# Fox layer on one core: weights split once for two token halves, h tiles loaded ahead on SP's queue, eight staging tiles

## The chip, the cores and the metric

The kernel runs on one core of one Trainium2 chip. The metric is the time on the device in microseconds; the kernel before took 2207.94 us (median of 3 runs, 2205.89 to 2215.18). The profile shown is of one further execution, which took 2212.18 us.

## The reference, cut to what matters

One layer (DEPTH is 1), so only the FoX mixer and the MLP run. S = 512 tokens, D = 2048, 16 heads of 128, MLP width 8192, all float32:

```
h = rmsnorm(x, g0)
q, k, v, f_pre = split(h @ w_in)                  # 2048 x (3 * 2048 + 16)
cum = cumsum(log_sigmoid(f_pre + b_f))            # per head, along the tokens
p = softmax(q k^T / sqrt(128) + cum_i - cum_j, causal)
x = x + rmsnorm(concat_heads(p @ v) @ w_out, g1)  # w_out 2048 x 2048
h = square(relu(rmsnorm(x, g2) @ w1))             # w1 2048 x 8192
x = x + rmsnorm(h @ w2, g3)                       # w2 8192 x 2048
```

## The kernel before, in words

**Split operands.** Every float32 operand of a large product is split in two: `hi` is the value cast to float32r on ScalarE, `lo` is value minus `hi`, subtracted on VectorE. A product is then three matmuls, hi x hi, hi x lo and lo x hi (`mm3`, lines 95 to 97; `mm3b`, lines 465 to 467). For weights of 128 x 1024 `load_split` issues the load on SP's queue (line 88) and does the cast (line 89) and the subtraction (line 90). Split operands stand in one large SBUF tile, `opr`, by column numbers that the code computes; raw weights wait in three tiles.

**Attention and output projection.** A loop over 16 heads multiplies q and k of one head while scores, transposes and values of the head before are slipped between the units. The result of a head is copied to `o32`; heads 0 to 9 (`KEEP = 10`) keep it in SBUF, heads 10 to 15 store it to the DRAM tile `od` (line 359) and load it again in `split_o` (line 399), which splits it (lines 401 and 402). The output projection has four groups of 512 columns (`NC = 4`), each with 8 weight tiles (`kb`), and accumulates four tiles of 128 tokens in PSUM. The last column group runs twice, once for each token half, and loads and splits its 8 weight tiles each time. During the second pass the first half is normalised (`norm1`, `residual`, `norm2`), stored to `x2d` by SP (line 527) and, at kb 6 and 7, transposed by `turn` (line 543).

**Plain tiles of the MLP.** The first 512 columns of w1 are multiplied plainly (`plain`), 8 weight tiles for each token half. The second pass keeps the split weights of three tiles and loads and splits the other five again. While it runs, `turn(1, p)`, `mix` and `split_mix` build the seven operands per pair of 128-row blocks of the input that the rest needs.

**The rest of the MLP, by Strassen-like sevens.** Columns of w1 come in pairs of 128 (30 pairs here); a pair of two-by-two blocks is multiplied with seven products in place of eight. `load_seven` loads four blocks of a weight (512 KB, SP, line 456) into one of four staging tiles of `spool`, forms three sums on VectorE (lines 457 to 459) and splits all seven (lines 440 and 441) into one of three places in turn (`tplaces`). One such weight is one step: 7 products x 2 x 3 = 42 matmuls. The first half (`ps`) takes 4 steps per pair and stores the squared relu in seven-form to DRAM (`hd`, line 693). The second half (`po`) goes over five blocks (`ci`) of six pairs (`CHUNK`), each with four column groups (`cp`): 24 steps per block. The h tile of a pair is loaded back by `want` (line 676, GpSimd's queue, one buffer `h7`) and split into one of eight places (`NRING`) of `opr`; six are in use in a block, two are spare. At the end of each column group seven PSUM banks are copied to `st` tiles (line 822, six buffers of `w2pool`) and stored to the DRAM tile `md`, from the second block on with accumulation (lines 824 and 826, GpSimd's queue). In the last block `gather` (line 773) reads the products of a finished column group back, two tiles of 896 KB which take staging tiles of `spool`, and adds them to `acc`; the gather of the last group, the last plain products (`pz`), the norm and the output follow the loop.

**Order.** All is written as straight code, with the slipped-in work placed by hand. On each engine's queue the instructions stand in the order that the scheduler of the language gave them; it follows the code, but takes an instruction that is free ahead of one that isn't.

## Time and profile before

| | us |
|---|---|
| median of 3 runs | 2207.94 |
| the profiled execution | 2212.18 |
| its span (first to last instruction) | 2210.4 |
| TensorE busy in it | 2130.7 (96%) |
| VectorE busy | 1498.8 (68%) |
| ScalarE busy | 953.0 (43%) |
| GpSimd busy | 267.9 (12%) |
| mean granted clock of TensorE, share of full speed | 0.985 |

The span is 1.78 us shorter than the profiled execution, which is 4.24 us above the median. Busy time of TensorE is from matmuls in a pipeline. By the granted clock TensorE ran at full speed nearly throughout. The stages: attention up to about 650 us, the output projection to 820, the plain tiles to 880, the first MLP half to 1494, the second to 2150, the tail to the end.

### The profile page before, as it was taken

The page shows a single profiled execution, that of the slowest core. Times are in us where ns is not written, and L with a number is a line of the kernel's source. Part 1 is how long each engine was busy: PE and PEld are TensorE (multiplying, and loading weights), DVE is VectorE, ACT ScalarE, POOL GpSimd, SP SyncE. Part 2 cuts the span into 40 slices and gives each one's busy share as a digit, 9 for nine tenths or more (in the row PEclk, how much of TensorE's full clock was granted, in tenths as well). Part 3 has the DMA queues.
Part 4 walks back from the last instruction along what each step waited for, and adds up shares of the span by engine and source line. Part 5 has one row for each costly group of instructions (what it writes and reads, how often), then busy time and mean ns, then how long its engine had stood idle before and what let it go on. Part 6 is the DMA issues. An engine that isn't in the chain of part 4 may idle for free. (4 is left out here: it accounts for less than half of the span.)

```text
span 2210.4 us, 34770 instructions
## 1 busy us (share of the span) xinstructions
PE 2130.7 (96%) x14450; PEld 1979.9 (90%) x14450; DVE 1498.8 (68%) x2004; ACT 953.0 (43%) x1138; POOL 267.9 (12%) x350
## 2 busy tenths in 40 slices
PE   8999999999989998999999999998999999999896
PEld 7788888888878878999999999998999999999885
DVE  9553453543543368888888888887687767767676
ACT  4433332333332365444444444445454555445352
POOL 8000000000010000000000000001112221222123
PEclk9999999999999999999999999999999999999998
DMA  5332232233343363544444444456567877877777
GB/s 175 110 95 82 93 95 89 95 93 103 91 152 99 121 229 124 179 162 163 150 156 163 162 144 163 162 167 211 196 218 194 217 205 183 225 182 197 190 206 225
DMA packets 103662, 346.12 MB, mean 157 GB/s; under 512 B 11712, under 2 KB 15936, under 8 KB 99024
## 3 DMA queue, kind: packets, MB, share of 16 engines
q1 hardware_dynamic: 72048, 232.42, 32.7%
q0 software_dynamic: 31312, 111.46, 18.6%
q8 instruction: 113, 1.85, 0.3%
q14 instruction: 45, 0.37, 0.1%
q10 hardware_dynamic: 144, 0.02, 0.0%
HBM read 264.65 MB, written 79.20 MB: 156 GB/s over the span
## 5 line engine op out<-in xcount | busy, mean ns | idle before, releaser
L466 PE MATMUL po<-opr 128*128 128x256 f32 x1204 | 344.7, 287 | 18.5 <-DVE opr L441 18.4
L465 PE MATMUL po<-opr 128*128 128x256 f32 x1204 | 341.1, 286 | 6.2 <-ACT opr L440 6.0
L467 PE MATMUL po<-opr 128*128 128x256 f32 x1204 | 340.4, 285 | 1.1 <-DVE opr L441 1.1
L465 PE MATMUL ps<-opr 128*128 128x256 f32 x1120 | 318.3, 284 | 6.6 <-ACT opr L440 6.6
L466 PE MATMUL ps<-opr 128*128 128x256 f32 x1120 | 318.1, 284 | 0.0
L467 PE MATMUL ps<-opr 128*128 128x256 f32 x1120 | 317.5, 284 | 0.2 <-DVE opr L441 0.2
L466 PEld LDWEIGHTS po<-opr 128*128 128x128 f32 x1204 | 234.2, 195 | 21.8 <-DVE opr L441 21.7
L465 PEld LDWEIGHTS po<-opr 128*128 128x128 f32 x1204 | 232.4, 194 | 7.8 <-ACT opr L440 7.0
L467 PEld LDWEIGHTS po<-opr 128*128 128x128 f32 x1204 | 232.6, 194 | 1.5 <-DVE opr L441 1.3
L465 PEld LDWEIGHTS ps<-opr 128*128 128x128 f32 x1120 | 216.2, 193 | 6.8 <-ACT opr L440 6.8
L466 PEld LDWEIGHTS ps<-opr 128*128 128x128 f32 x1120 | 216.3, 193 | 0.0
L467 PEld LDWEIGHTS ps<-opr 128*128 128x128 f32 x1120 | 215.8, 193 | 0.5 <-DVE opr L441 0.5
L441 DVE TENSOR_TENSOR opr<-seven_a,opr 128x1792 fp32r<-128x1792 f32 x80 | 161.9, 2024 | 51.5 <-ACT opr L440 50.2
L440 ACT CAST opr<-seven_b 128x1792 fp32r<-128x1792 f32 x86 | 145.1, 1693 | 115.5 <-PE po L467 88.2
L440 ACT CAST opr<-seven_a 128x1792 fp32r<-128x1792 f32 x80 | 134.8, 1685 | 139.0 <-PE ps L466 133.4
L441 DVE TENSOR_TENSOR opr<-seven_b,opr 128x1792 fp32r<-128x1792 f32 x86 | 173.7, 2020 | 19.8 <-ACT opr L440 19.6
L457 DVE TENSOR_TENSOR seven_b<-seven_b 128x512 f32<-128x512 f32 x120 | 82.6, 688 | 125.5 <-DMA seven_b<-in_w2s 125.1
L465 PE MATMUL ps<-opr,w 128*128 128x256 f32 x560 | 158.5, 283 | 0.0
L466 PE MATMUL ps<-opr,w 128*128 128x256 f32 x560 | 158.5, 283 | 0.0
L467 PE MATMUL ps<-opr,w 128*128 128x256 f32 x560 | 158.5, 283 | 0.0
L465 PE MATMUL po<-w,opr 128*128 128x256 f32 x476 | 136.3, 286 | 3.5 <-ACT w L440 2.3
L466 PE MATMUL po<-w,opr 128*128 128x256 f32 x476 | 136.2, 286 | 1.8 <-DVE w L441 1.8
(233 smaller groups left out, 5233.1 us busy)
## 6 DMA issues: line engine op xcount, KB each, us to landing
seven_a<-in_w1s SPq DMA_DIRECT2D x120, 512.0 KB, 3.6
seven_b<-in_w2s SPq DMA_DIRECT2D x120, 512.0 KB, 4.3
md<-st POOLq DMA_DIRECT2D x140, 256.0 KB, 8.4
hd<-ev POOLq DMA_DIRECT2D x30, 1024.0 KB, 4.4
h<-hd POOLq DMA_DIRECT2D x30, 896.0 KB, 5.2
raw_o<-in_wo SPq DMA_DIRECT2D x40, 512.0 KB, 3.5
raw_q<-in_wq SPq DMA_DIRECT2D x32, 512.0 KB, 3.7
raw_k<-in_wk SPq DMA_DIRECT2D x32, 512.0 KB, 3.7
```

The lines of the kernel that those rows point to most:

```text
L440: nc.scalar.copy(hi, z)
L441: nc.vector.tensor_tensor(out=lo, in0=z, in1=f32(hi), op=ALU.subtract)
L457: nc.vector.tensor_tensor(out=raw[:, 4:6], in0=raw[:, 1:3], in1=raw[:, 0:1].to_broadcast([P, 2, 256]), op=ALU.add)
L465: nc.tensor.matmul(o, a[0], b[0], start=start, stop=False, skip_group_check=True)
L466: nc.tensor.matmul(o, a[0], b[1], start=False, stop=False, skip_group_check=True)
L467: nc.tensor.matmul(o, a[1], b[0], start=False, stop=stop, skip_group_check=True)
```

## The change

- `KEEP`, `od` and its stores and loads go: every head's result keeps a tile of its own in SBUF. `cb`, the row of sums of a head, has one buffer in place of two.
- The last column group of the output projection splits its 8 weight tiles once, into places `OPLACE` of `opr` that stay for both token halves. The plain tiles split all 8 weight tiles once, into `PPLACE`; the first token half takes them in the order `EARLY`, the second from 0 to 7.
- The split inputs move within `opr`; `split_mix` writes two pieces (256 and 768 columns), each with a cast and a subtraction.
- `want` becomes `h_load` (SP's queue) and `h_split`, called by `h_steps` at given steps counted from the start of a block. Tiles 1 and 3 of the first block are loaded into staging tiles of `spool`, the others into the one `h7` tile. The places of h in `opr` follow `HSLOT`. The first step of the MLP sevens starts with the third of the three places for split weights.
- The order of the four weights of pair 2 is 0 to 3.
- `st` has eight buffers. `gather` of groups 0 and 1 is called two column groups later at their first step, that of group 2 after the loop.

```diff
-    def load_split(src, name, pieces=1, between=None):
-        wplace[0] += 1
-        at = WBASE + wplace[0] % 3 * 2048
+    def load_split(src, name, pieces=1, between=None, at=None):
+        if at is None:
+            wplace[0] += 1
+            at = WBASE + wplace[0] % 3 * 2048
...
-                cb = ap_.tile([P, S], F32, tag="cb", name=f"cb_{h}", bufs=2)
+                cb = ap_.tile([P, S], F32, tag="cb", name=f"cb_{h}")
...
-                if h < KEEP:
-                    o32[h] = ap_.tile([P, S], F32, tag=f"o32_{h}", name=f"o32_{h}")
-                    nc.scalar.copy(o32[h], ps)
-                    return
-                o = ap_.tile([P, S], F32, tag="o32", name=f"o32_{h}", bufs=4)
-                nc.scalar.copy(o, ps)
-                nc.sync.dma_start(od[h], o)
+                o32[h] = ap_.tile([P, S], F32, tag=f"o32_{h}", name=f"o32_{h}")
+                nc.scalar.copy(o32[h], ps)
...
+        OPLACE = [20480, 22528, 24576, 26624, 18432, WBASE, WBASE + 2048, WBASE + 4096]
+        w_last = {}
         def out_unit(py, c, kb, ts=range(TT)):
-            w = load_split(wo[c, kb], f"o{c}_{kb}")
+            if c < NC - 1:
+                w = load_split(wo[c, kb], f"o{c}_{kb}")
+            else:
+                if kb not in w_last:
+                    w_last[kb] = load_split(wo[c, kb], f"o{c}_{kb}", at=OPLACE[kb])
+                w = w_last[kb]
...
         def split_mix(p, m4):
-            hi, lo = opr[:, p * 2560 + 256:p * 2560 + 1280], opr[:, p * 2560 + 1536:p * 2560 + 2560]
-            nc.scalar.copy(hi, m4)
-            nc.vector.tensor_tensor(out=lo, in0=m4, in1=f32(hi), op=ALU.subtract)
+            for at, n, c in ((p * 1024 + 256, 512, slice(0, 256)), (RB + p * 1536, 768, slice(256, 1024))):
+                w = c.stop - c.start
+                hi, lo = opr[:, at:at + w], opr[:, at + n:at + n + w]
+                nc.scalar.copy(hi, m4[:, c])
+                nc.vector.tensor_tensor(out=lo, in0=m4[:, c], in1=f32(hi), op=ALU.subtract)
...
+        EARLY = [5, 6, 7, 4, 0, 1, 2, 3]
+        PPLACE = [18432, WBASE, WBASE + 2048, WBASE + 4096, RB, RB + 2048, RB + 4096, RB + 6144]
...
         def plain(hf, p):
-            order = LATE if hf else range(8)
-            if hf == 0 or p < 5:
-                w[p] = load_split(w1p[p], f"a{hf}_{p}")
+            order = range(8) if hf else EARLY
+            if hf == 0:
+                w[p] = load_split(w1p[p], f"a_{p}", at=PPLACE[EARLY.index(p)])
...
+    tplace[0] = 1
...
-    def want(n):
-        if n >= NSTR:
-            return
-        h7 = h_tile(f"h7_{n}")
-        nc.gpsimd.dma_start(h7, hd[n, :, 256:2048].rearrange("p (n c) -> p n c", c=256))
-        at = n % NRING * 2 * SLOT
-        hops[n] = split7(h7, [opr[:, at + i * SLOT:at + (i + 1) * SLOT] for i in range(2)])
+    HSLOT = [0, 3, 6, 1, 2, 4, 5, 7]
+    hraw = {}
+    def h_load(n):
+        hraw[n] = seven(f"h7_{n}") if n in (1, 3) else h_tile(f"h7_{n}")
+        nc.sync.dma_start(hraw[n], hd[n, :, 256:2048].rearrange("p (n c) -> p n c", c=256))
+    def h_split(n):
+        at = HSLOT[n % NRING] * 2 * SLOT
+        hops[n] = split7(hraw[n], [opr[:, at + i * SLOT:at + (i + 1) * SLOT] for i in range(2)])
+    def h_steps(i):
+        for ci in range(NSTR // CHUNK):
+            if ci == 0:
+                splits, loads = [-3, -2, -1, 0, 1, 2], [-4, -4, -3, -2, -1, 1]
+            else:
+                splits, loads = [-16, -11, -5, -3, -1, 2], [-18, -13, -7, -5, -3, 0]
+            for k in range(CHUNK):
+                if i == ci * 4 * CHUNK + splits[k]:
+                    h_split(ci * CHUNK + k)
+            for k in range(CHUNK):
+                if i == ci * 4 * CHUNK + loads[k]:
+                    h_load(ci * CHUNK + k)
...
-        w2pool = w2s_.enter_context(tc.tile_pool(name="w2pool", bufs=6, reuse_waits="tile"))
+        w2pool = w2s_.enter_context(tc.tile_pool(name="w2pool", bufs=8, reuse_waits="tile"))
...
-                    if ci == 0 and cp == 0 and k < 3:
-                        want(k + 3)
-                    elif ci > 0 and cp == 0 and k in (0, 2):
-                        want(n0 + 4 + k // 2)
-                    if cp in (1, 2) and k == 2:
-                        want(n0 + CHUNK + cp - 1)
-                    if cp == 3 and k in (2, 4):
-                        want(n0 + CHUNK + 1 + k // 2)
+                    h_steps((ci * 4 + cp) * CHUNK + k)
...
-                        if cp > 0 and k == 5:
-                            gather(cp - 1, ep, seven)
+                        if cp > 1 and k == 0:
+                            gather(cp - 2, ep, seven)
...
+        gather(2, ep3, lambda name: big(name)[:, 0:7])
         gather(3, ep3, lambda name: big(name)[:, 0:7])
```

## Rows read from the trace of the kernel before

**Rows 1.** Page, part 1: engine, busy us (share of the span) xinstructions.

```profile
PE 2130.7 (96%) x14450; PEld 1979.9 (90%) x14450; DVE 1498.8 (68%) x2004; ACT 953.0 (43%) x1138; POOL 267.9 (12%) x350
```

**Rows 2.** Busy time by stage: from:to length, engines (xinstructions), clock, DMA share, GB/s.

```profile
580.00:640.00 60.00, 60.00 (x293) 50.63 (x292) 34.47 (x60) 25.64 (x50) 7.02 (x13) 1.00 0.36 110
640.00:680.00 40.00, 33.48 (x142) 27.15 (x141) 12.38 (x17) 10.52 (x16) 2.13 (x4) 0.91 0.46 141
...
780.00:820.00 40.00, 35.08 (x175) 29.08 (x174) 26.63 (x46) 23.04 (x47) 4.30 (x8) 0.96 0.72 249
...
860.00:900.00 40.00, 28.63 (x207) 27.34 (x207) 36.94 (x53) 22.17 (x30) 1.63 (x3) 0.87 0.52 193
900.00:1480.00 580.00, 580.00 (x4836) 580.00 (x4835) 493.79 (x666) 259.64 (x202) 14.93 (x28) 1.00 0.47 156
1488.00:1540.00 52.00, 44.57 (x336) 43.35 (x335) 39.18 (x45) 26.44 (x22) 6.42 (x12) 0.93 0.63 210
...
1640.00:2020.00 380.00, 370.19 (x3049) 367.79 (x3048) 284.04 (x310) 188.68 (x173) 85.06 (x103) 1.00 0.77 201
2020.00:2147.00 127.00, 113.13 (x870) 110.19 (x869) 87.29 (x118) 52.52 (x49) 25.11 (x28) 0.95 0.74 199
```

**Rows 3.** Timeline of PE: start, us, what [idle before <- releaser].

```profile
659.97 0.79 PE L95 MATMUL py<-opr 128*128 128x512 f32 x1 [5.33 <-ACT opr L401]
...
805.42 0.50 PE L95 MATMUL py<-opr 128*128 128x512 f32 x1 [2.89 <-ACT opr L89]
...
886.70 0.58 PE L465 MATMUL ps<-opr 128*128 128x256 f32 x1 [6.62 <-ACT opr L440]
...
1518.66 0.39 PE L465 MATMUL po<-opr 128*128 128x256 f32 x1 [1.77 <-ACT opr L440]
...
2082.61 0.58 PE L466 MATMUL po<-opr 128*128 128x256 f32 x1 [4.62 <-DVE opr L441]
```

**Rows 4.** Waits, whole span: who <- whom: us in total, times, longest.

```profile
ACT opr L401 <- DMA o<-od: 9.0, 2, 7.7
...
POOL h L676 <- DVE opr L441: 226.9, 29, 11.5
...
ACT opr L440 <- DMA h<-hd: 78.9, 17, 8.6
...
ACT st L822 <- DMA md<-st: 50.4, 18, 4.8
...
PE ph L97 <- DVE opr L90: 4.5, 4, 1.6
```

**Rows 5.** Groups by line: what xcount | busy us, mean ns | idle before.

```profile
L441 DVE TENSOR_TENSOR opr<-h,opr 128x1792 fp32r<-128x1792 f32 x30 | 60.6, 2021 | 6.3 <-ACT opr L440 6.3
...
L440 ACT CAST opr<-h 128x1792 fp32r<-128x1792 f32 x30 | 50.8, 1692 | 83.8 <-DMA h<-hd 78.9 <-PE po L466 4.9
...
L90 DVE TENSOR_TENSOR opr<-raw_a,opr 128x1024 fp32r<-128x1024 f32 x13 | 15.9, 1221 | 3.9 <-PE ph L96 1.9 <-ACT opr L89 1.7
```

**Rows 6.** Page, part 6: DMA issues, KB each, median us to landing.

```profile
seven_b<-in_w2s SPq DMA_DIRECT2D x120, 512.0 KB, 4.3
md<-st POOLq DMA_DIRECT2D x140, 256.0 KB, 8.4
...
h<-hd POOLq DMA_DIRECT2D x30, 896.0 KB, 5.2
```

**Rows 7.** Timeline of SP, output projection and plain tiles.

```profile
790.05 3.96 SPq L527 DMA_DIRECT2D x2d<-yg  x6
...
865.97 23.33 SPq L456 DMA_DIRECT2D seven_a<-in_w1s  x5
```

**Rows 8.** Timeline of DVE behind the loop.

```profile
2170.71 0.43 DVE L776 TENSOR_TENSOR m<-m 128x256 f32<-128x256 f32 x1 [8.85 <-DMA m<-md]
```

**Rows 9.** Timeline of POOL at the start of the second MLP half.

```profile
1513.03 0.53 POOL L676 DMA_DIRECT2D h<-hd  x1 [6.42 <-DVE opr L441]
1522.89 0.53 POOL L676 DMA_DIRECT2D h<-hd  x1 [9.34 <-DVE opr L441]
```

More of the change, by code (lines that the diff above doesn't have):

```diff
@@ L33 @@
 CHUNK = 6
-KEEP = 10
 WARM = 9
@@ L161, in fox_layer @@
     cumd = dpool.tile([H, S], F32, name="cumd")
-    od = dpool.tile([H, P, S], F32, name="od")
     with ExitStack() as att:
@@ L395, in split_o @@
         def split_o(h):
[L396 to L399 removed]
+            o = o32[h]
             ah, al = act_pair()
@@ L474, in xop @@
             at, step = RA + p * 1024 + i * 256, 512
+        elif i < 4:
+            at, step = p * 1024 + (i - 2) * 256, 512
         else:
-            at, step = p * 2560 + (i - 2) * 256, 1280
+            at, step = RB + p * 1536 + (i - 4) * 256, 768
         return opr[:, at:at + 256], opr[:, at + step:at + step + 256]
@@ L557, in turn @@
                 nc.scalar.activation(x4[:, 512 + 256 * i:768 + 256 * i], ps[:, 256 * i:256 * (i + 1)], AF.Copy, scale=gc[:, 1, k:k + 1])
-            at = p * 2560
+            at = p * 1024
             nc.scalar.copy(opr[:, at:at + 512], x4[:, 512:1024])
-            nc.vector.tensor_tensor(out=opr[:, at + 1280:at + 1792], in0=x4[:, 512:1024], in1=f32(opr[:, at:at + 512]), op=ALU.subtract)
+            nc.vector.tensor_tensor(out=opr[:, at + 512:at + 1024], in0=x4[:, 512:1024], in1=f32(opr[:, at:at + 512]), op=ALU.subtract)
             return x4
@@ L627, in plain @@
                 else:
-                    at = p * 2560 + (256 if kh == 0 else 0)
-                    b = opr[:, at:at + 256], opr[:, at + 1280:at + 1536]
+                    b = xop(p, 3 - kh)
                 for f in range(4):
@@ L632, in plain @@
                     mm3(ph[f][:, cols], a, b, p == order[0] and kh == 0, p == order[-1] and kh == 1)
-        for p in range(8):
-            plain(0, p)
-            if p == 0:
-                norm1(1)
-            if p < 4:
-                residual(1, p)
-            if p == 3:
-                norm2(1)
-            if p >= 4:
-                store_x2(1, p - 4)
-        x4, m4 = {}, {}
-        for i in range(3):
-            x4[i] = turn(1, LATE[i])
-            if i < 2:
-                m4[i] = mix(LATE[i], x4[i])
-        for i in range(8):
-            plain(1, LATE[i])
-            split_mix(LATE[i], m4[i])
-            if i + 2 < 8:
-                m4[i + 2] = mix(LATE[i + 2], x4[i + 2])
-            if i + 3 < 8:
-                x4[i + 3] = turn(1, LATE[i + 3])
+        for i in range(8):
+            plain(0, EARLY[i])
+            if i == 0:
+                norm1(1)
+            if i < 4:
+                residual(1, i)
+            if i == 3:
+                norm2(1)
+            if i >= 4:
+                store_x2(1, i - 4)
+        x4, m4 = {}, {}
+        for p in range(3):
+            x4[p] = turn(1, p)
+            if p < 2:
+                m4[p] = mix(p, x4[p])
+        for p in range(8):
+            plain(1, p)
+            split_mix(p, m4[p])
+            if p + 2 < 8:
+                m4[p + 2] = mix(p + 2, x4[p + 2])
+            if p + 3 < 8:
+                x4[p + 3] = turn(1, p + 3)
     first.close()
@@ L724, in fox_layer @@
             b = [(psum_att if n % 2 else psum_acc)(f"ps_{n}_{i}") for i in range(4)]
-            order = [3, 2, 0, 1] if n == 2 else range(4)
-            for g in order:
+            for g in range(4):
                 w = load_seven(w1s[n - 2, g], f"a{n}_{g}")
@@ L731, in fox_layer @@
                         mm3b(b[bi][:, part * 256:(part + 1) * 256], [zz[:, BOF[j], kk * P:(kk + 1) * P] for zz in w], xop(2 * g + kk, AOF[j]),
-                             g == order[0] and kk == 0 and FIRST[bi] == j, g == order[-1] and kk == 1)
-                if n == 2 and g in order[1:3]:
-                    evac_plain(order.index(g) - 1)
-                if n == NPAIR - 1 and g > 0:
-                    want(g - 1)
+                             g == 0 and kk == 0 and FIRST[bi] == j, g == 3 and kk == 1)
+                if n == 2 and g in (1, 2):
+                    evac_plain(g - 1)
+                if n == NPAIR - 1:
+                    h_steps(g - 4)
             evac_seven(b, n)
@@ L747, in last_w @@
         nc.sync.dma_start(raw, w2p[i // 2, i % 2])
-        hi, lo = opr[:, i * 2048:i * 2048 + 1024], opr[:, i * 2048 + 1024:i * 2048 + 2048]
+        at = [0, 10752, 21504, 23552, 2048, 4096, 6144, 8192][i]
+        hi, lo = opr[:, at:at + 1024], opr[:, at + 1024:at + 2048]
         nc.scalar.copy(hi, raw)
```

13 lines of the change are left out of this document (4 added, 9 removed).

## The prediction

> **What bounds the kernel now.** The reader starts with the shares of the engines on the page: TensorE is busy for 2130.7 of 2210.4 us [rows 1], so what a change can win is its idle time, about 80 us, and what the clock loses beside it. The second view is the busy time by stage [rows 2]. In the first half of the MLP (900 to 1480 us) TensorE is never idle: 4836 matmuls in 580 us, 0.12 us each, so one step (one weight tile, 7 products x 2 x 3 matmuls = 42) takes 5.04 us. The same holds up to 640 us. The loss sits in six places, each read as the stage's length less the busy time, and as the stage's length times what the granted clock lacks (mean clock 0.91 over 40 us: at most 3.6 us of full-speed work lost; between the levels of 1.2 and 2.4 GHz the clock falls after the idle places and comes back): end of attention (640 to 680) 6.5 idle + 3.6 clock; last columns of the output projection (780 to 820) 4.9 + 1.6; end of the plain tiles and hand-over to the MLP (860 to 900) 11.4 + 5.2; start of the second MLP half (1488 to 1540) 7.4 + 3.6; its middle (1640 to 2020) 9.8 + 0; its end (2020 to 2147) 13.9 + 6.4. Together about 54 us idle and 20 us of clock. The rest, behind 2147, is the tail, in which VectorE waits 8.85 us for the last gathered products [rows 8].
>
> The third view, the idle times of TensorE one by one [rows 3], names who ends each: a cast of ScalarE (L401) at 660, a cast of w_out (L89) at 805, a cast of a MLP tile (L440) at 886 and at 1518, the subtraction behind it (L441) at 2082. ScalarE is itself only 43% busy, so the fourth view asks what it waits for [rows 4]: 9.0 us for `o<-od`, 78.9 us for `h<-hd`, 50.4 us for `md<-st` to free a staging tile.
>
> **Part 1: heads 10 to 15 stay in SBUF.** Six stores and six loads of 256 KB go, and with them the waits of L401. The idle 5.33 us at 660 ends with that cast [rows 3], and the 9.0 us say that it waited for the loads [rows 4]. What is late next is the chain of head 15 (copy, cast, subtraction): it hangs on the value matmuls, which stand three units ahead of its use, each 48 matmuls long. I take 9.5 of the 10.1 us; bounds 6 and 10. The room is paid with one `cb` tile in place of two: the load of a head's row of sums then starts when VectorE has read the row of the head before, still a head's matmuls ahead of its use. TensorE is full there (60.00 of 60 us [rows 2]), so I take nothing. Were the cover gone, 15 loads of 256 KB, each below the 4.3 us that 512 KB take [rows 6], would be at most 65 us.
>
> **Part 2: w_out's last columns and the plain tiles are split once.** For the second token half 8 loads, 8 casts and 8 subtractions of w_out go, and 5 of each of the plain tiles (13 subtractions of 1.22 us [rows 5], 16 us of VectorE, and 13 casts). At 780 to 820 TensorE waits for just these: SP issues six `x2d` stores at 790 to 794 [rows 7], which wait for VectorE, ahead of the last two loads of w_out; the idle 2.89 us at 805 [rows 3] follows. In the new kernel no load stands there: 4.9 + about 1 of clock, 6 us in all (bounds 3 and 6.5). In the plain tiles' second pass 4.5 us of waits for L90 [rows 4] go, since no L90 is left in it. VectorE is busy for 36.94 of 40 us there [rows 2]; it loses 5 x 1.22 and gains 8 more instructions by the two-piece `split_mix`: from 0.43 us for 256 columns, 1.22 for 1024 and 2.02 for 1792 [rows 5, 8] an extra instruction costs some 0.16 us, 1.3 in all, so VectorE is ahead by 4.8 us. The hand-over at 886 (6.62 us) [rows 3] waits for the first MLP tile, whose load SP issues only at 865.97 [rows 7], behind the plain loads that now go; its first split now has a place that is free early (`tplace` starts at the third). But its sums still share VectorE with the last `split_mix`: I take half, 3.3 us, and 3 of the 5.2 us of clock. 4.5 + 3.3 + 3 = 11 (bounds 4 and 16). The new places of x, h and the last weights in `opr`, and the plain order of the first MLP steps, change no instruction's size; a place that came free too late would show as a cast waiting for TensorE, and I take nothing for it. Part 2 gives 17 us.
>
> **Part 3: h loads ahead, on SP's queue.** Before, an h tile is loaded when the one before it has been split (one buffer): GpSimd's queue waits 226.9 us for that in 29 of 30 loads [rows 4]. At the start of the second half the issues at 1513.03 and 1522.89 [rows 9] are 9.9 us apart, a step is 5.04: h tiles 2 to 5 can't keep up, and TensorE idles 7.4 us. Now tiles 1 and 3 use the weights' staging tiles, so two loads of six no longer hang in that chain. What is late next is VectorE: six subtractions of 2.02 us [rows 5] beside the weights' work, 39.18 of 52 us [rows 2], and two of four staging tiles are lent out. Of 11 us I take 7 (bounds 0 and 10). Later h tiles still have one buffer, so there the load can't start earlier than before; what changes is the ring: `md<-st` takes 8.4 us to land and stood ahead of h on GpSimd's queue (h: 5.2) [rows 6].
>
> **Part 4: eight staging tiles.** Seven copies leave PSUM at the end of each column group; with six tiles the seventh waits for the first store, 50.4 us in 18 waits, 2.8 each [rows 4], and every cast queued behind it on ScalarE waits too. With eight the seven copies of a group fit, and the next group comes six steps, 30 us, later. Split weights have three places, so ScalarE is at most two steps ahead of TensorE, and 2.8 us less is as much as most of the idle times there. Parts 3 and 4 in the middle: 7 of 9.8 us (bounds 1 and 9.8). At the end: the gathers of column groups 0 and 1 move to a step where their products have long landed, and group 2's leaves the loop; but each still takes two of four staging tiles, for which the loads of weights wait (the 4.62 us at 2082 [rows 3]), and now stands beside seven stores. Of 20.3 us I take 8 (bounds -3 and 15).
>
> **Part 5: the tail.** Group 2's gather (two loads of 896 KB, 14 additions of 0.43 us) now falls behind the loop, into the 8.85 us [rows 8] in which VectorE waits anyway, but its loads share the DMA engines with the last stores, which are on the path. Loads of h's size take 5.2 us [rows 6]; hidden they cost nothing, both in a row 10 us. I take 3 us lost.
>
> **The sum.** 9.5 + 17 + 7 + 7 + 8 - 3 = 45.5 us. The profiled execution took 2212.2 (span 2210.4 and 1.8 around it): 2166.7. It lies 4.2 above the median 2207.94, so I forecast 2162. 0.5% (11 us) is about what a measurement of this kernel can tell from no change.
>
> **A rule against part 3.** h waits for its transfer, 78.9 us in all [rows 4], and h lands in 5.2 us while 512 KB of weights land in 4.3 [rows 6]. By the Trainium skill (DMA: Bandwidth & Descriptors, "Issuing engines are not separate DMA queues") all queues run on the same 16 DMA engines and another queue only saves time on the sequencer. By that rule the h waits would stay; the rows agree in so far as the landing is about proportional to size. This would be rival A.
>
> **The rivals.** A: the second MLP half keeps its losses, because the waits for h and for weights are waits for transfers, which are not fewer. For it: each later h still has one buffer. Against: ScalarE's 50.4 us for `md<-st` are a wait for a tile, and that goes. Then 9.5 + 17 - 3 = 23.5 remain: 2188.7, or 2184 against the median. Chance 0.22.
>
> B, slower: SP's queue stops. At each of the four changes from one block of six h tiles to the next, the load of tile 3 waits for the split of tile 2, which waits until TensorE has left the place that it overwrites. If the weight load of the next step stands behind it on SP, it comes after cast and subtraction (1.69 + 2.02 [rows 5]), lands 4.3 later [rows 6], and needs sums (1.5 for their 1024 columns by the same rows as the 0.16), a cast and a subtraction: 3.7 + 0.7 + 4.3 + 1.5 + 3.7 = 13.9 us after that step's end, where TensorE has 5.04 us of work left. 9 us idle and some 2.5 of clock (6.4 stand beside the 13.9 us idle of the end [rows 2]), four times, 46 us, against 23.5 gained: 2235, or 2230. It decides if SP keeps the order of the code. Against: SP doesn't; in rows 7 six stores go ahead of loads that stand before some of them in the code, as each came free. Chance 0.06.
>
> C, more: all 54 us idle and most of the clock go, the tail costs nothing: 68 us, 2140. Against: VectorE at 36.94 of 40 us and the lent staging tiles. Chance 0.12.
>
> D: parts 1 and 2 fall short as well, because VectorE bounds the plain tiles and the hand-over and a little of the wait at the end of attention stays: their lower bounds 6 + 3 + 4, and 3 lost in the tail, 10 us gained, 2198. Chance 0.05.
>
> **Numbers.** The forecast has 0.55, with 2150 to 2177 as its own range. From C's 2140 to A's and D's side, with the bounds of the end and the tail, 2138 to 2194 holds 8 in 10. Faster by over 0.5% (below 2197): the forecast, C, most of A, half of D: 0.87. Within 0.5%: the rest of A and D, 0.07. Slower: B, 0.06.
>
> **What would show it.** Right: no idle TensorE at 650 to 660 and no `od`; no L88 load in the second pass of w_out's last columns; TensorE's first matmul of a seven some 23 us earlier than 886.7; `md<-st` gone from ScalarE's waits; h waits of ScalarE clearly below 78.9. Wrong: SP's waits before `seven_b` ended by an h split, TensorE idle for 5 us or more at block changes, the last gather landing more than 5 us later behind the loop's end, TensorE's idle time between 1640 and 2147 as before.

## The result, and the profile after

The changed kernel takes 2180.6 us (median of 4 runs, 2180.0 to 2183.1) against 2208.1 of the kernel before (4 runs): a ratio of 0.9872, 95% interval 0.9849 to 0.9896, 27.5 us. The forecast was 2162 with a range of 2138 to 2194: the sign and the range held, but 45.5 us were forecast of one profile against the other, and 32.2 came (span 2210.4 to 2178.2).

Where they came from is read off TensorE's timeline, at the starts of four kinds of products: plain tiles (`ph`), sevens of the first MLP half (`ps`), sevens of the second (`po`), and the end of the last `po`. All runs of this study stand in one table, stage lengths in us; what follows refers to it.

```
                           to first  plain +   first   second   tail    span   ratio to before
                           ph        hand-over half    half             (95% interval)
before                     820.7     66.0      607.9   655.6    60.2   2210.4  1
after                      805.5     60.9      607.5   637.3    67.0   2178.2  0.9872 (0.9849-0.9896)
e1 heads to DRAM           814.7     60.9      607.5   641.3    67.1   2191.5  0.9897 (0.9877-0.9917)
e2 plain loads again       806.7     62.9      607.0   641.0    67.0   2184.7  0.9864 (0.9845-0.9882)
e3 six staging tiles       805.7     60.9      607.6   641.9    67.2   2183.3  0.9893 (0.9875-0.9911)
e4 h on GpSimd's queue     806.0     61.0      608.0   656.7    66.9   2198.7  0.9925 (0.9908-0.9941)
e5 ring of three           811.6     67.0      607.0   636.1    67.0   2188.8  0.9914 (0.9897-0.9932)
e6 gather 2 in the loop    805.3     61.0      607.7   647.4    58.6   2180.0  0.9849 (0.9828-0.9871)
e7 multiply on VectorE     804.1     61.5      607.1   637.4    59.1   2169.1  0.9835 (0.9810-0.9859)
e8 sums first              806.6     58.3      607.9   635.7    67.1   2175.6  0.9845 (0.9824-0.9866)
e9 = e7 + e8               804.2     59.3      608.0   638.9    59.0   2169.4  0.9801 (0.9782-0.9820)
e10 own tile, last weights 804.4     58.2      607.6   640.3    76.2   2186.7  0.9885 (0.9865-0.9904)
e11 = e9 + gather 2 in loop 806.5    58.2      607.8   638.6    57.7   2168.7  0.9794 (0.9775-0.9814)
e12 = e11 + third place    803.7     58.3      608.5   638.5    58.5   2167.6  0.9821 (0.9804-0.9837)
```

How far a stage scatters from one profile to another is seen where nothing of it was edited: the first column 803.7 to 806.7, the second half 635.7 to 641.3, the tail (with GpSimd's multiplications) 66.9 to 67.2. So 15 us were won before the plain tiles, 5 in them, none in the first half, 18 in the second, and 7 were lost in the tail.

Two columns scatter mostly in one part. In the first it is the part ahead of the output projection, whose first product stands at 617.6 to 620.6 us; from there to the first plain product every run in which nothing of it was edited takes 186.1 us (before: 202.5). In the second half it is the last four of the twenty column groups of 252 products:

```
                           first 16 groups   last 4 groups
before                     510.1             145.5
after                      490.1             147.2
e3, e6 (six staging tiles) 497.3, 497.9      144.6, 149.5
e4 (h on GpSimd's queue)   504.9             151.9
the other nine             489.2 to 492.9    144.5 to 150.4
```

So the half was won in its first sixteen groups (20 us), and nothing was won in the last four. The ratios in the first table are over all executions, the stages from one profiled execution each: that of e3 is the fastest of its four, those of e4 and e6 are the slowest of six and of four.

Part 1 of the page, which answers to [rows 1]: TensorE is busy for 9 us less only; what went is idle time and clock.

```profile
PE 2121.5 (97%) x14450; PEld 1975.6 (91%) x14450; DVE 1488.9 (68%) x1999; ACT 943.1 (43%) x1133; POOL 252.2 (12%) x320
```

The busy time by stage, which answers to [rows 2] (each stage moved ahead to about the same products; columns as there).

```profile
640.00:680.00 40.00, 40.00 (x181) 33.29 (x180) 12.42 (x15) 11.29 (x19) 4.25 (x8) 1.00 0.47 151
780.00:820.00 40.00, 39.79 (x263) 36.38 (x262) 31.43 (x65) 26.56 (x63) 4.29 (x8) 1.00 0.64 222
860.00:900.00 40.00, 33.29 (x258) 33.00 (x259) 35.89 (x53) 20.27 (x21) 1.09 (x2) 0.91 0.49 170
1474.00:1526.00 52.00, 49.43 (x395) 48.82 (x394) 46.63 (x52) 31.04 (x26) 4.26 (x8) 0.97 0.74 245
1626.00:1980.00 354.00, 352.86 (x2941) 352.65 (x2940) 268.58 (x295) 182.58 (x169) 75.23 (x85) 1.00 0.80 208
1980.00:2111.00 131.00, 118.18 (x899) 114.76 (x899) 86.02 (x110) 58.62 (x59) 25.61 (x30) 0.95 0.67 176
```

The end of the attention and the last columns of the projection are full, at full clock. The start of the second half lost 7.4 + 3.6 us, now 2.6 + 1.6; its middle 9.8, now 1.1; its end 13.9 + 6.4, now 12.8 + 6.6: that stage is as it was.

TensorE's timeline, which answers to [rows 3]: the 5.33 and 2.89 us are gone, the hand-over is not, and the end has new waits of the old kind.

```profile
866.44 0.58 PE L464 MATMUL ps<-opr,w 128*128 128x256 f32 x1 [6.73 <-ACT w L439]
...
1985.54 0.38 PE L464 MATMUL po<-opr 128*128 128x256 f32 x1 [1.24 <-ACT opr L439]
```

The waits of the whole span, which answer to [rows 4]: `o<-od` and `st <- md<-st` no longer occur, and the waits for h fell from 78.9 to

```profile
ACT opr L439 <- DMA h<-hd: 56.9, 21, 5.4
```

Two of the groups by line, which answer to [rows 5]: instructions as long as before, 8 splits of plain tiles in place of 13.

```profile
L439 ACT CAST opr<-h 128x1792 fp32r<-128x1792 f32 x30 | 50.9, 1696 | 69.4 <-DMA h<-hd 56.9 <-PE po L465 11.0 <-PE ps L466 1.5
...
L90 DVE TENSOR_TENSOR opr<-raw_a,opr 128x1024 fp32r<-128x1024 f32 x8 | 9.7, 1219 | 6.4 <-ACT opr L89 6.4
```

The page's DMA issues, which answer to [rows 6]: h lands no faster on SP's queue than it did on GpSimd's (5.2).

```profile
seven_b<-in_w2s SPq DMA_DIRECT2D x120, 512.0 KB, 4.4
md<-st POOLq DMA_DIRECT2D x140, 256.0 KB, 9.1
...
h<-hd SPq DMA_DIRECT2D x30, 896.0 KB, 5.3
```

SP's timeline at the plain tiles, which answers to [rows 7]: the first MLP tile, issued at 865.97 before, is issued 43 us ahead of its use.

```profile
819.36 0.33 SPq L455 DMA_DIRECT2D seven_a<-in_w1s  x1
```

VectorE's timeline in the tail, which answers to [rows 8]: the 8.85 us wait for gathered products has become 3.91 us, but an addition of 128x256 lasts 6.74 us.

```profile
2126.97 0.42 DVE L800 TENSOR_TENSOR m<-m 128x256 f32<-128x256 f32 x1 [3.91 <-DMA m<-md]
...
2130.48 6.74 DVE L800 TENSOR_TENSOR m<-m 128x256 f32<-128x256 f32 x1 [0.47 <-issue]
2137.15 0.41 DVE L801 TENSOR_TENSOR acc<-m 128x256 f32<-128x256 f32 x1
```

SP's timeline at the start of the second half, which answers to [rows 9]: h loads of one buffer are still 9.9 us apart, but the sixth and last tile of the first block is now loaded 11.7 us behind the first product of the half (1473.9; the first line), before 28.3 us behind it (1494.6; the second of [rows 9]). The second line is already the next block's first tile.

```profile
1485.63 0.33 SPq L683 DMA_DIRECT2D h<-hd  x1
...
1495.54 0.33 SPq L683 DMA_DIRECT2D h<-hd  x1
```

### The profile page after: what moved, and what is told of

Same layout as the page of the kernel before. It is cut to its first block, busy times and chain, and to the rows that moved or that the text cites. A ratio compares the mean times of both kernels' runs of the same rounds, so it can differ in the third digit from the quotient of the medians.

```text
span 2178.2 us, 34778 instructions
## 1 busy us (share of the span) xinstructions
PE 2121.5 (97%) x14450; PEld 1975.6 (91%) x14450; DVE 1488.9 (68%) x1999; ACT 943.1 (43%) x1133; POOL 252.2 (12%) x320
## 3 DMA queue, kind: packets, MB, share of 16 engines
q0 software_dynamic: 26992, 83.93, 14.8%
## 5 line engine op out<-in xcount | busy, mean ns | idle before, releaser
L456 DVE TENSOR_TENSOR seven_b<-seven_b 128x512 f32<-128x512 f32 x120 | 82.5, 689 | 114.4 <-DMA seven_b<-in_w2s 113.8
L843 POOL DMA_DIRECT2D md<-st x112 | 99.6, 1799 | 355.8 <-ACT st L839 355.8
L464 PE MATMUL po<-w,opr 128*128 128x256 f32 x476 | 134.3, 284 | 1.7 <-DVE ev L739 1.1
```

Source lines behind the costliest of these rows:

```text
L456: nc.vector.tensor_tensor(out=raw[:, 4:6], in0=raw[:, 1:3], in1=raw[:, 0:1].to_broadcast([P, 2, 256]), op=ALU.add)
L464: nc.tensor.matmul(o, a[0], b[0], start=start, stop=False, skip_group_check=True)
L843: nc.gpsimd.dma_start(md[cp, :, j], st, accum_op=ALU.add)
```

## The experiments

All start from the changed kernel, unless another is named.

**e1: six heads' outputs to DRAM again.**

```diff
+                if h < KEEP:
                     o32[h] = ap_.tile([P, S], F32, tag=f"o32_{h}", name=f"o32_{h}")
...
+                nc.sync.dma_start(od[h], o)
```

> The changed kernel with its attention part undone: six of the sixteen heads' outputs again go to DRAM after the attention and are loaded back for the output projection, and the tile of cumulated gates has two buffers again. Everything else is the changed kernel (2180.6 us). Theory: the 12.0 us by which the changed kernel reaches its first evacuation of the output projection earlier (678.1 to 666.1 us) are these loads; nothing later makes them up, so the run takes 2189 to 2193 us and its first such evacuation stands near 678 us. Rival 1: what the loads cost is only what the forecast took from the stall rows, 9.5 us (6 to 10): 2187 to 2190 us. Rival 2: the 12 us come from elsewhere in the change (the places of the split weights): 2179 to 2183 us.

The first plain product stands at 814.7 us, 9.1 later than in the changed kernel, and all later stages but the scattering second half keep their lengths. Counted from the projection's first product, where the scatter is gone, its second column group starts after 57.5 us before, 48.4 in the changed kernel and 57.1 in e1: 9.1 us were won, and e1 gives 8.7 back. The wait of [rows 3] is there again:

```profile
661.24 0.80 PE L96 MATMUL py<-opr 128*128 128x512 f32 x1 [4.88 <-ACT opr L401]
```

Rival 1, the forecast's term, is right. At the first evacuation, the theory's mark, 13 us are won by the same count; 4 of them are gone when the second group starts.

**e2: five plain tiles loaded and split again, into their own places.**

```diff
-            if hf == 0:
+            if hf == 0 or p < 5:
```

> The changed kernel, but five of the eight plain weight tiles are loaded and split a second time for the second token half, into the place where they already are (the result is the same). Theory: between the first and the last plain product the changed kernel gained 5.2 us (15.2 to 20.4 us ahead), and that is all that these loads cost: 2184 to 2187 us, with waits for the split weights back in the stretch 840 to 860 us. Rival 1, the forecast's term: 11 us with the hand-over and the clock, 2190 to 2193 us, the idle time before the first of the seven products growing past 6.7 us. Rival 2: VectorE, busy 19.07 of 20 us there, is what bounds this stretch; five more subtractions of 1.2 us then cost all their 6 us and push the hand-over too: 2187 to 2190 us.

Neither theory nor rivals: the plain pass (first to last `ph`) takes 54.3 us as against 54.2, and only the hand-over behind it grows, from 6.73 to 8.63 us. The repeated loads, casts and subtractions were not what the pass had waited for.

```profile
869.62 0.58 PE L464 MATMUL ps<-opr,w 128*128 128x256 f32 x1 [8.63 <-ACT w L439]
```

**e5: the weights in a ring of three places again, loaded for each half.** It asks what then had been waited for.

```diff
-            if hf == 0:
-                w[p] = load_split(w1p[p], f"a_{p}", at=PPLACE[EARLY.index(p)])
+            w[p] = load_split(w1p[p], f"a{hf}_{p}")
```

(and the same for `out_unit`'s last columns)

> The changed kernel with the weights of the projection's last columns and of the plain tiles loaded and split for each token half again, each time into the next of the three rotating places, as in the kernel before (there five of the eight plain tiles were repeated, here all eight). The run e2, which repeated the plain loads in places of their own, moved the start of the first seven products by only 2.0 us against the first plain product. Theory: what the change removed is the wait for a free place among three, more than the loads: the last product of the projection comes 5 to 7 us later (near 808 us in place of 802.2), and from the first plain product to the first of the seven it takes 65 to 68 us again (60.9 in the changed kernel, 62.9 in e2, 66.0 before); 2188 to 2194 us in all. Rival (the repeated loads, casts and subtractions are the cost): 2 to 4 us at each of the two, 63 to 64 us from plain to seven, 2184 to 2187 us.

The theory held at both places: 811.6 to the first plain product (+6.1, the forecast's 6) and 67.0 us from there to the sevens; the pass takes 61.1 us (59.4 before, with five repeated tiles). e5's waits, in the form of [rows 4], have the one back that the forecast counted as 4.5.

```profile
PE ph L97 <- DVE opr L90: 6.2, 5, 1.7
```

With e2 this says: in the plain pass what cost time was having three places in turn, not that there were more splits. e5 repeats eight tiles; at five repeated ones the comparison is 59.4 us before, with three places, and 54.3 in e2, with places of their own. In e5 ScalarE's casts wait both for a place (3.5 us in 3) and for raw tiles that are loaded late (5.7 us in 5); which of the two costs more was not separated.

**e3: six staging tiles.**

```diff
-        w2pool = w2s_.enter_context(tc.tile_pool(name="w2pool", bufs=8, reuse_waits="tile"))
+        w2pool = w2s_.enter_context(tc.tile_pool(name="w2pool", bufs=6, reuse_waits="tile"))
```

> The changed kernel with six staging tiles instead of eight for the sums of the second MLP half. Theory: the waits of ScalarE for a staging tile (50.4 us in 18 before, none after) come back, and with them the idle time of TensorE at the starts of chunks (7.4 and 3.6 us in the first, of which 2.6 us are left): 2186 to 2191 us. Rival: what cured those waits is that the h loads left GpSimd's queue, so that the stores are issued sooner; then six tiles are enough: 2180 to 2183 us and no more than 10 us of such waits.

The waits are back, more of them than before (50.4), and the first sixteen groups take 497.3 us, in e6, which has six tiles too, 497.9, against 489.2 to 492.9 with seven or eight. So the staging tiles are worth 4 to 9 us, as the theory said (2188.8 us, the median of e3, lies in its range), and the rival falls. The loss isn't at the start of the half, though: its first group takes 33.7 us in e3, 35.1 in the changed kernel. The 641.9 us of the whole half hide the loss, since its last groups came out short in this profile.

```profile
ACT st L839 <- DMA md<-st: 64.2, 19, 5.2
```

**e4: h loads on GpSimd's queue.**

```diff
-        nc.sync.dma_start(hraw[n], hd[n, :, 256:2048].rearrange("p (n c) -> p n c", c=256))
+        nc.gpsimd.dma_start(hraw[n], hd[n, :, 256:2048].rearrange("p (n c) -> p n c", c=256))
```

> The changed kernel with its loads of h issued on GpSimd's queue instead of SyncE's, at the same places of the code. Theory: one h load landed in 5.3 us on SyncE's queue and in 5.2 us on GpSimd's before, so the queue is not faster; but on GpSimd the loads stand behind stores that wait for ScalarE's copies, and come late at the starts of chunks: 2184 to 2190 us, with waits of ScalarE for h well over the 56.9 us of the changed kernel. Rival (what counts is that the loads are issued more steps ahead, not the queue): 2179 to 2183 us, waits for h within 10 us of 56.9.

The second half takes 656.7 us in this profile, the slowest execution of e4. Its first sixteen groups take 504.9 us, 12 to 16 more than in the runs with eight or seven staging tiles and h on SP's queue, and by the ratios e4 stands 0.53% (12 us) behind the changed kernel. So most of that half's gain is gone, the rival falls, and the waits for h are there as the theory had them:

```profile
h<-hd POOLq DMA_DIRECT2D x30, 896.0 KB, 5.5
...
ACT opr L439 <- DMA h<-hd: 95.3, 22, 11.5
```

But the theory's reason is not what the trace shows. Of the 27 h loads that follow a split, 25 are issued within 0.5 us of its end, one after 1.0 us, and only one, after 4.0 us, behind stores. The stores don't stand behind h loads either: they are issued 0.5 us behind ScalarE's copies (median; 2.4 at most), in the changed kernel 0.4 (1.7). What the sixteen groups lose, 14.8 us against the changed kernel, is lost in two of them: the ninth takes 35.0 us and the thirteenth 38.8, in place of 30.2. In each of these two an h load follows seven accumulating stores on the same queue and lands 12.4 and 12.7 us after its issue; the same two loads land in 9.1 and 7.9 us on SP's queue. GpSimd, ScalarE and TensorE in the ninth group of e4,

```profile
1722.71 6.26 POOL L843 DMA_DIRECT2D md<-st  x7
1732.14 0.56 POOL L683 DMA_DIRECT2D h<-hd  x1 [3.16 <-DVE opr L440]
...
1744.53 1.69 ACT L439 CAST opr<-h 128x1792 fp32r<-128x1792 f32 x1 [10.16 <-DMA h<-hd]
...
1751.06 0.58 PE L465 MATMUL po<-opr 128*128 128x256 f32 x1 [2.81 <-DVE opr L440]
```

and ScalarE in the changed kernel at the same load:

```profile
1738.12 1.69 ACT L439 CAST opr<-h 128x1792 fp32r<-128x1792 f32 x1 [5.43 <-DMA h<-hd]
```

By the Trainium skill (DMA: Bandwidth & Descriptors, "Issuing engines are not separate DMA queues") another engine saves only the time to start a transfer. The medians of the landing agree (5.5 and 5.3 us); these two loads do not. Why they land late behind stores of their own queue is not shown.

**e6: the third gather back in the loop, with six staging tiles.**

```diff
+                        if cp == 3 and k == 5:
+                            gather(2, ep, seven)
...
-        gather(2, ep3, lambda name: big(name)[:, 0:7])
```

> The changed kernel with the gather of the third column group back at the end of the loop, where it stood before, and, for the room that this takes, six staging tiles: to be compared with e3 (the changed kernel with six staging tiles: 637.3 + 4.6 us from the first to the last product of the second MLP half, 67.2 us from there to the end). Theory: the gather behind the loop is what made the tail longer; its end comes 60 to 62 us after the last product, and the loop keeps its length to 2 us: 5 to 7 us below e3. Rival 1: in the loop the gather takes two of four staging tiles, and the loop becomes 4 us or more longer, so that nothing is won. Rival 2: the tail is longer because GpSimd's multiplications hold VectorE up, wherever the gather stands: the tail stays at 65 us or more.

The theory holds for the tail, which is 8.6 us shorter than e3's, and by the ratios e6 is 0.44% (10 us) faster than e3. Its loop is 5.5 us longer in these two profiles, which rival 1 would explain by the lent tiles, but the first sixteen groups are alike, and the last four, 149.5 us with the wait below and 144.6 in e3, lie in the scatter: rival 1 is not borne out. Rival 2 falls: the additions that were held up are no longer beside the multiplications.

```profile
2015.53 0.58 PE L465 MATMUL po<-opr 128*128 128x256 f32 x1 [4.46 <-DVE opr L440]
```

**e7: the multiplications by g on VectorE.**

```diff
-                if i < n - 1:
-                    nc.gpsimd.tensor_tensor(out=y, in0=y, in1=g, op=ALU.mult)
-                else:
-                    nc.vector.tensor_tensor(out=y, in0=y, in1=g, op=ALU.mult)
+                nc.vector.tensor_tensor(out=y, in0=y, in1=g, op=ALU.mult)
```

> The changed kernel with the tail's thirteen multiplications by g (on GpSimd, 1.25 us each in a row) on VectorE, where they take 0.6 us each, 7.8 us in all. In the changed kernel one addition of the gather took 6.74 us in place of 0.42, from 2130.5 to 2137.2, while GpSimd made five multiplications in a row (2130.7 to 2136.9). Theory: VectorE is held up by those; then this addition takes 0.42 us, the gathers end some 6 us sooner, and with the other long ones gone too the tail gets 3 to 6 us shorter than its 67.0 us in spite of the 7.8 us: 2174 to 2178 us. Rival: that addition waits for its transfer, which lands at about that time; then it stays as late, and VectorE's 7.8 us more come on top: 2183 to 2188 us.

The tail takes 59.1 us in place of 67.0, a larger gain than expected, although VectorE does 13 instructions more. VectorE's groups by line in the tail (busy us, mean ns | idle before), first of the changed kernel,

```profile
L895 DVE SCALAR_TENSOR_TENSOR acc<-acc,r,x 128x512 f32<-128x512 f32 (+1 forms) x17 | 16.4, 1022 | 0.1
L880 DVE TENSOR_TENSOR acc<-pz,acc 128x512 f32<-128x512 f32 (+1 forms) x16 | 10.3, 646 | 13.2 <-PE pz L97 13.2
L800 DVE TENSOR_TENSOR m<-m 128x256 f32<-128x256 f32 x4 | 9.0, 2246 | 4.4 <-DMA m<-md 3.9 <-issue 0.5
```

then of e7:

```profile
L892 DVE SCALAR_TENSOR_TENSOR acc<-acc,r,x 128x512 f32<-128x512 f32 (+1 forms) x17 | 11.1, 710 | 0.0
...
L880 DVE TENSOR_TENSOR acc<-pz,acc 128x512 f32<-128x512 f32 (+1 forms) x16 | 10.2, 644 | 11.1 <-PE pz L97 11.1
L800 DVE TENSOR_TENSOR m<-m 128x256 f32<-128x256 f32 x4 | 1.7, 420 | 0.5 <-DMA m<-md 0.3
```

The gather's first additions fall from 2246 to 420 ns, the last step from 1022 to 710; the addition from PSUM keeps its 646.

**e8: the first MLP tiles' sums ahead of the plain tiles' evacuation on VectorE.**

```diff
+                    with tc.issue_after(last_sum[0].ins):
-                    evac_plain(g - 1)
+                        evac_plain(g - 1)
```

(`last_sum` is the last sum of the tile loaded just before)

> The changed kernel with one order pinned on VectorE: the evacuation of the plain tiles' first half (three instructions, 1.5 us) comes behind the sums of the first and second MLP tile, and the one of the second half behind those of the third; nothing else moves. In the changed kernel TensorE idles 6.73 us before the first of the seven products, ended by a cast at 864.7 us, and VectorE makes those sums at 862.9, behind the last split of the plain inputs (to 860.6) and that evacuation. Theory (VectorE's order sets this wait; the tile has landed by 855): the sums begin near 860.6, the idle time falls to 4.0 to 4.7 us, and the run takes 2177 to 2179 us. Rival (the tile's load is late, as the forecast had it): the idle time stays at 6.3 us or more, 2180 to 2183 us.

The theory held: 4.17 us idle, and 2.6 us less from the plain tiles to the sevens. VectorE's timeline of the changed kernel, with the wait that stood ahead of the sums (L456),

```profile
861.79 0.69 DVE L714 TENSOR_TENSOR ev<-ev 128x512 f32<-128x512 f32 x1 [1.20 <-ACT ev L710]
...
862.86 0.68 DVE L456 TENSOR_TENSOR seven_a<-seven_a 128x512 f32<-128x512 f32 x1
```

and of e8, where they (L458 there) follow the last split at once:

```profile
860.29 1.29 DVE L583 TENSOR_TENSOR opr<-m,opr 128x768 fp32r<-128x768 f32 x2 [0.90 <-ACT opr L582]
861.50 0.68 DVE L458 TENSOR_TENSOR seven_a<-seven_a 128x512 f32<-128x512 f32 x1
```

**e9: e7 and e8 together.** Their two diffs, nothing else.

> The changed kernel with both edits that gave time: the tail's multiplications on VectorE (e7: tail 59.1 us in place of 67.0) and the sums of the first MLP tiles ahead of the plain tiles' evacuation (e8: 4.2 us idle in place of 6.73). They lie 1250 us apart. Theory: the gains add up, 7.9 + 2.6 us: 2169 to 2173 us, a ratio to the kernel before of 0.982 to 0.984. Rival: the start of the second MLP half is set by something that does not move with the hand-over, so e8's 2.6 us are lost there: the first product of the second half stands no earlier than 1473 us, ratio 0.9835 as e7.

The two gains stand beside each other in the table (59.3 and 59.0 us): 0.9801 (0.9782 to 0.9820). The rival falls: the first product of the second half stands at 1471.5 us.

**e10: e9, with a staging tile of its own for the last weights, and the second of the last h loads later.**

```diff
-        raw = seven(f"raw_z{i}").rearrange("p n c -> p (n c)")[:, 0:1024]
+        raw = rz[0].tile([P, 1024], F32, tag="raw_z", name=f"raw_z{i}")
...
-                        if cp == 0 and k in (4, 5):
-                            last_h(k - 4)
+                        if (cp, k) in ((0, 4), (1, 1)):
+                            last_h(cp)
```

> As e9, and at the end of the loop: the eight last plain weights are staged in a tile of their own (one buffer) in place of two of the four staging tiles of the sevens, and the second of the two last h loads comes three steps later, so that ScalarE does not stand before it (11.46 us at 1982.9 in the changed kernel, TensorE idle for 1.24 and 1.83 us right behind). To be compared with e9; the stretch from the first to the last product of the second half took 637.3 us in the changed kernel, with 12.8 us idle in its last 137. Theory (the stretch waits because the staging tiles are lent): the idle times near 1986 us go, those behind 2060 shrink by half or more, 631 to 634 us. Rival (the loads of the stretch share DMA engines that are full: 188 GB/s over 2000 to 2110 us, busy in nearly all slices): 636 to 639 us.

The loop doesn't gain (640.3 us), and with one buffer the last weights come so late that the tail takes 76.2 us. TensorE's timeline:

```profile
2087.95 0.58 PE L467 MATMUL po<-opr 128*128 128x256 f32 x1 [4.04 <-DVE opr L440]
...
2120.65 1.22 PE L95 MATMUL pz<-opr 128*128 128x512 f32 x2 [3.34 <-ACT opr L777]
```

**e11: e9 with the third gather in the loop.** The diff of e6, and

```diff
-        w2pool = w2s_.enter_context(tc.tile_pool(name="w2pool", bufs=8, reuse_waits="tile"))
+        w2pool = w2s_.enter_context(tc.tile_pool(name="w2pool", bufs=7, reuse_waits="tile"))
```

> As e9, with the gather of the third column group back at the end of the loop and seven staging tiles (room comes from two constant tiles moved). In e6 that place cost 5.5 us in the loop against e3 and gave back 8.7 us in the tail, where GpSimd still multiplied. Theory: most of what the gather cost behind the loop was the hold-up by GpSimd, which is gone in e9 (tail 59.1 us): the tail now gets only 2 to 5 us shorter, the loop 4 to 6 us longer, the sum within 3 us of e9. Rival: the gather and its two loads are on the tail's path by themselves: tail 50 to 53 us, 3 to 5 us faster than e9.

Tail 57.7 in place of 59.0, loop 638.6 and 638.9: the sum is within 3 us, as the theory said, but neither part moved as far as it had them (tail 2 to 5 us shorter, loop 4 to 6 longer). Once GpSimd doesn't multiply, it matters little where that gather stands. This is the fastest kernel of the study, 0.9794, with e9 inside its interval.

**e12: e11 with a third place for split weights to the end.**

```diff
-                                tplaces.pop()
+                                tplaces[2] = [opr[:, i:i + SLOT] for i in (17920, 19712)]
```

> As e11, but the split weights keep three places for the last eighteen steps. In the changed kernel, and in the one before, the third place is given up after the sixth step of the last block of h (its memory goes to the gathered sums); here it moves into the slot of an h tile that is no longer used, and for that the second of the two last h loads, and with it its wait on ScalarE near 1983 us, moves to the last column group, and the last plain weights move by one place each. To be compared with e11: from the first to the last product of the second half 638.6 us, in whose last 137 us TensorE idles 12.5 us at a lowered clock. Theory: with two places ScalarE can cast the next weight tile only when TensorE has left the one before (44.9 us of such waits in 11 behind 1975 us), and VectorE's subtraction behind it comes late; with three the idle time falls to 5 us or less and the stretch to 628 to 633 us: 2157 to 2163 us. Rival 1 (VectorE's gathers between the weights' sums and subtractions are what is late): 636 to 640 us, 2165 to 2170 us. Rival 2 (the loads, at 188 GB/s, are late): the same length, and VectorE's waits for the weights' transfer (24.9 us in 10 in the changed kernel) stay or grow.

The loop keeps its length (638.5), and by the ratios e12 is no faster than e11: the theory falls. VectorE's waits for the weights' transfer stay (24.3 us in 10 in e11), as rival 2 has it, in the waits of 1975 to 2112 us:

```profile
DVE seven_b L459 <- DMA seven_b<-in_w2s: 25.8, 9, 8.3
```

But the loads land no slower there than in the middle of the half (median 4.2 us, 4.7 in the middle), so rival 2's late transfers are rather loads issued late: SP waits for a staging tile, in e12 28.4 us in 4 waits for VectorE's subtractions. In e10, with two places, ScalarE waits for a place instead, 60.0 us in 12. Full DMA engines, the rival of e10, are not likely either: in the changed kernel their share is 0.67 at the end and 0.80 in the middle, where TensorE idles 1.1 us. Both edits at once, with two buffers for the last weights, were not tried; what bounds the end of the loop stays open.

## Why the prediction fell short

**Attention: right.** 9.5 forecast, 9.1 came, 8.7 of it by e1.

**Last columns of the projection: right in size.** 6 forecast, with 6.5 as the upper bound; 7.4 came (145.0 us before, 137.6 after, from the second column group to the plain tiles), 6.7 of it by e5. e5 undoes the places and the loads together, so which of them it is was not separated there.

**Plain pass: size right, reason incomplete.** 4.5 forecast, 5.2 came (59.4 to 54.2 us). "No L90 is left" suggested that the work was the cost; e2 puts the work back and loses nothing in the pass, e5 puts the three places back and loses 6.9 us.

**Hand-over: the first step that failed.** The prediction said that the hand-over "waits for the first MLP tile, whose load SP issues only at 865.97", and took half of 6.62 us and 3 of clock. The load did move to 819.36, where such loads land within 5.1 us, and the idle time is 6.73. The other half of its own sentence was the whole: the sums wait on VectorE, behind the last `split_mix` (to 860.6 us) and behind an instruction of the evacuation that itself waits 1.20 us. e8 shows 2.6 of the 6.7 us to be order alone; the 4.17 us left there are the end of that split, the three sums and a cast of 1.69 us. The kernel before had the same order, and its trace could have shown it: the load issued at 865.97 landed at 870.5, and VectorE came to the sums (L457) 12.6 us later.

```profile
882.00 0.69 DVE L690 TENSOR_TENSOR ev<-ev 128x512 f32<-128x512 f32 x1 [0.97 <-ACT ev L686]
...
883.07 0.68 DVE L457 TENSOR_TENSOR seven_a<-seven_a 128x512 f32<-128x512 f32 x1
```

**Second half, start and middle: the right parts, too small a sum.** 7 and 7 forecast. By idle time and clock of the stages 6.9 and 8.7 came; by their products the first sixteen groups became 20.0 us shorter. The credit was given to parts 3 and 4 together: e3 and e6 give 4 to 9 us to the staging tiles, e4 12 to 16 to the queue.

**End of the loop: the second step that failed.** 8 of 20.3 us forecast; nothing came (145.5 us before, 147.2 after, by idle time and clock 0.8 us). The prediction doubted it itself (two of four staging tiles lent, gathers beside stores) and took 8 between -3 and 15 without a row that gave it; e10 and e12 show two single cures that do nothing.

**Tail: the third, a term of the right sign and the wrong mechanism.** 3 us for shared DMA engines forecast, 6.8 lost. The gather's additions came to stand beside GpSimd's multiplications; in the kernel before VectorE stood idle during such a run, in the 8.85 us of [rows 8]:

```profile
2164.88 5.04 POOL L866 TENSOR_TENSOR acc<-acc,g3b 128x512 f32<-128x512 f32 x4
```

Taking the multiplications away gives 7.9 us (e7). Without them the moved gather costs 1.3 us (e9 against e11), which is what is left for the forecast's term.

Together: 0.4 us short up to the plain tiles, 5.4 in these and the hand-over with its clock, 9.7 at the end of the loop, 3.8 in the tail, and 6.0 more than forecast in the first sixteen groups: 45.5 - 19.3 + 6.0 = 32.2. Against the median the miss is 18.6 us, 5.3 more, mostly because the profile before stood 4.2 us above its median and the one after 0.6 below.

That the range held is in part luck: misses of both signs were added up, 2180.6 lies outside the 2150 to 2177 that the forecast itself was given, and it is nearest to rival A's 2184, whose mechanism failed (18.3 us of the second half went, though h lands as before). B fails too (354 us across the block changes lose 1.1), C and D lie 40 us below and 17 us above the result. In the rule against part 3 one reading was wrong: 896 KB are 1.75 times 512 KB and landed in 1.2 times the time (5.2 and 4.3 us), so the landing is not proportional to size.

## What to carry to other kernels

When a load is moved ahead of a stall, follow the tile one step further, through the queue of the engine that handles it next: it may stand there behind work that nobody waits for. Before an instruction is moved into an idle place, look at what the other engines do at that time, not only at the DMA queues. Here the term for which the trace gave no row, the end of the loop, brought nothing; such a term deserves the lower half of its bounds. And before a change is read off two profiles, find the part of a stage that scatters in unedited runs and count the rest by its products: 7 us of the staging tiles were hidden by the last groups' scatter.

## What the runs showed of the hardware

GpSimd and VectorE held each other up. GpSimd's timeline of the changed kernel, beside the 6.74 us of 2130.48 above:

```profile
2130.66 6.27 POOL L884 TENSOR_TENSOR acc<-acc,g3b 128x512 f32<-128x512 f32 x5
2140.79 2.57 POOL L884 TENSOR_TENSOR acc<-acc,g3b 128x512 f32<-128x512 f32 x1 [3.85 <-ACT pz L881]
```

VectorE's addition began 0.18 us before five multiplications in a row (1.25 us each) and ended just behind the last, 6.74 us in place of 0.42. The next multiplication fell into a run of VectorE's additions of 0.41 us and took 2.57 us itself. The Trainium skill (SBUF — State Buffer, "Who interferes with whom") says that a VectorE instruction with two inputs in SBUF contends with a GpSimd instruction that reads SBUF, and one with at most one SBUF input, outside the modes that use two ports, doesn't. The traces agree: the addition held up had two inputs in SBUF, and in the kernel before an addition with one input in PSUM lay wholly inside three multiplications and kept its 0.41 us.

```profile
2199.87 3.35 POOL L866 TENSOR_TENSOR acc<-acc,g3b 128x512 f32<-128x512 f32 x3 [2.64 <-ACT pz L863]
...
2201.10 0.41 DVE L862 TENSOR_TENSOR acc<-pz,acc 128x256 f32<-128x256 f32 x1
```

(The means of such additions in the tail, 646 and 644 ns, say less: in the changed kernel only one of them falls beside a multiplication, and for 0.23 us.) What the trace adds is that one instruction of VectorE can be kept out by a whole run of GpSimd's.
